# Rotary embedding on one core: x's first megabyte ahead of sin on the sync queue, and the first tile in fewer pieces

## The chip, the cores and the metric

The kernel runs on one core of a Trainium2 chip. The metric is the device time of one execution in microseconds, the median over the runs. Every time inside an execution comes from one profiled execution and is counted from the start of its span.

## The reference

`x` has the shape (8, 2048, 8, 64): batch, sequence, heads, head size, in float32. `cos` and `sin` have the shape (2048, 32). The two halves of each head are rotated by the tables of their position:

```python
x1 = x[..., : x.shape[-1] // 2]
x2 = x[..., x.shape[-1] // 2 :]
cos = cos[None, :, None, :]
sin = sin[None, :, None, :]
out1 = x1 * cos - x2 * sin
out2 = x1 * sin + x2 * cos
return np.concatenate([out1, out2], axis=-1)
```

The input and the output are 33.55 MB each, and each table is 256 KB.

## The kernel before

**Tiles.** A partition q holds the 16 positions 16q to 16q + 15, so the tables lie on the chip as 128 rows of 16 x 32 values (2 KB in each partition). One batch entry is cut into two slabs of 8 positions. A slab is 128 x 4096 float32, which is 2 MB in rows of 16 KB. There are 16 slabs: the first half of the positions for all 8 batch entries, then the second half. `HD` is 512, the values of one position; `UNIT` is 4 positions or 2048 values; `SLAB` is 4096.

**Loads.** `load(i)` issues slab i's load on the sync queue (SP). `cuts(i)` says in how many transfers: slab 0 in four (256 KB, 256 KB, 512 KB and 1 MB), all others in one. Ten slabs have a buffer (`NBUF`). In front of all of this the sync queue issues the load of `sin_sb` (L86) and the scalar queue (ACT) the load of `cos_sb` (L87). Loads 10 to 15 are issued inside the main loop, each when the buffer of the slab ten places earlier has been stored.

**Tables.** ScalarE writes `nsin`, the negative of sin (L91). VectorE (DVE) copies cos into PSUM as `cos_ps` (L92).

**Work on one piece.** `rotate(i, lo, n)` takes n values of a slab. `pieces(i)` says how slab i is cut for this: slab 0 into 512, 512, 1024 and 2048, the last slab into 2048, 1024, 512 and 512, all others into two units of 2048. For each piece

- GpSimd (POOL) writes `t2` with two multiplications on half of the values each (L107): the first halves of the heads by sin, then the second halves by nsin. A piece of 2048 is therefore 1024 elements in each of the two. There are three buffers of `t2`, in SBUF.
- DVE multiplies the piece by cos into `t1` (L112; one buffer, in PSUM), and adds `t2` to it, writing over the piece of x (L117).

When a slab is done, ACT issues its store (L127), as one transfer of 2 MB; the last slab is stored piece by piece.

**Order.** The engines run side by side, and each one works through its own instructions in a fixed order, waiting on semaphores for its inputs and free buffers. That order is set when the program is built, and can differ from the order of the calls in the source where two instructions don't depend on each other. On the DMA side, sync carries all loads but cos, and scalar carries cos and all stores.

Of the kernel before, what the change touches and what calls it, by code (L numbers as in the profile page):

```python
# [2 lines left out]

# [4 lines left out]


@with_exitstack  # L10
def kernel(
    ctx: ExitStack,
    tc: tile.TileContext,
    x: bass.AP,
    cos: bass.AP,
    sin: bass.AP,
    out: bass.AP,
):
    nc = tc.nc
    f32 = mybir.dt.float32  # L20
    PSUM = bass.MemoryType.PSUM

    B, S, H, D = x.shape
    Dh = D // 2
    P = 128
    HD = H * D
    R = S // P

    SL = 8
    n_half = R // SL  # L30
    SLAB = SL * HD
    UNIT = 4 * HD
    NBUF = 10

    xv = x.rearrange("b (q r) h d -> b q (r h d)", q=P)
    ov = out.rearrange("b (q r) h d -> b q (r h d)", q=P)
    cos_src = cos.rearrange("(q r) d -> q r d", q=P)
    sin_src = sin.rearrange("(q r) d -> q r d", q=P)

    const_pool = ctx.enter_context(tc.tile_pool(name="const", bufs=1))  # L40
    tab_pool = ctx.enter_context(tc.tile_pool(name="tab", bufs=1, space=PSUM))
    t1_pool = ctx.enter_context(tc.tile_pool(name="t1p", bufs=1, space=PSUM))
    xpool = ctx.enter_context(tc.tile_pool(name="xpool", bufs=NBUF))
    t2_pool = ctx.enter_context(tc.tile_pool(name="t2p", bufs=3))

    cos_sb = const_pool.tile([P, R, Dh], f32, tag="cb")
    sin_sb = const_pool.tile([P, R, Dh], f32, tag="sb")
    nsin = const_pool.tile([P, R, Dh], f32, tag="ns")
    cos_ps = tab_pool.tile([P, R, Dh], f32, tag="cp")

    slabs = [(b, l) for l in range(n_half) for b in range(B)]
    last = len(slabs) - 1
    xts = {}

    def cuts(i):
        if i == 0:
            return [HD, HD, 2 * HD, UNIT]
        return [SLAB]

    def pieces(i):  # L60
        if i == 0:
            return [HD, HD, 2 * HD, UNIT]
        if i == last:
            return [UNIT, 2 * HD, HD, HD]
        return [UNIT, UNIT]

    def stores(i):
        return pieces(i) if i == last else [SLAB]

    def spans(sizes):  # L70
        lo = 0
        for n in sizes:
            yield lo, n
            lo += n

    def load(i):
        b, l = slabs[i]
        xt = xpool.tile([P, SLAB], f32, tag="xt", name=f"xt{i}")
        for lo, n in spans(cuts(i)):
            nc.sync.dma_start(  # L80
                out=xt[:, lo : lo + n],
                in_=xv[b, :, l * SLAB + lo : l * SLAB + lo + n],
            )
        xts[i] = xt

    nc.sync.dma_start(out=sin_sb, in_=sin_src)  # L86
    nc.scalar.dma_start(out=cos_sb, in_=cos_src)  # L87
    for i in range(NBUF):
        load(i)

    nc.scalar.mul(nsin, sin_sb, -1.0)  # L91
    nc.vector.tensor_copy(cos_ps, cos_sb)  # L92

    def rep(a, n):
        return dataclasses.replace(a, ap=[a.ap[0][:], a.ap[1][:], [0, n], a.ap[-1][:]])

    def rotate(i, lo, n):
        b, l = slabs[i]
        xt = xts[i][:, lo : lo + n]
        r0 = l * SL + lo // HD  # L100
        nr = n // HD
        t1 = t1_pool.tile([P, n], f32, tag="t1")
        t2 = t2_pool.tile([P, n], f32, tag="t2")
        xu = xt.rearrange("p (g u d) -> p g u d", u=2, d=Dh)
        t2u = t2.rearrange("p (g u d) -> p g u d", u=2, d=Dh)
        for u, tab in ((1, sin_sb), (0, nsin)):
            nc.gpsimd.tensor_mul(  # L107
                out=t2u[:, :, u, :].rearrange("p (r h) d -> p r h d", h=H),
                in0=xu[:, :, 1 - u, :].rearrange("p (r h) d -> p r h d", h=H),
                in1=rep(tab[:, r0 : r0 + nr, :], H),  # L110
            )
        nc.vector.tensor_mul(  # L112
            out=t1.rearrange("p (r k d) -> p r k d", r=nr, d=Dh),
            in0=xt.rearrange("p (r k d) -> p r k d", r=nr, d=Dh),
            in1=rep(cos_ps[:, r0 : r0 + nr, :], 2 * H),
        )
        nc.vector.tensor_add(out=xt, in0=t1, in1=t2)  # L117

    for i, (b, l) in enumerate(slabs):
        done = 0  # L120
        st = list(spans(stores(i)))
        for lo, n in spans(pieces(i)):
            rotate(i, lo, n)
            done = lo + n
            while st and st[0][0] + st[0][1] <= done:
                slo, sn = st.pop(0)
                nc.scalar.dma_start(  # L127
                    out=ov[b, :, l * SLAB + slo : l * SLAB + slo + sn],
                    in_=xts[i][:, slo : slo + sn],
                )  # L130
        if i >= 1 and i - 1 + NBUF <= last:
            load(i - 1 + NBUF)


# [1 line left out]
_INS = ['x', 'cos', 'sin']  # L136
_OUTS = [((8, 2048, 8, 64), 'float32')]


# [23 lines left out]
```

## Time and profile before

| what | value |
|---|---|
| median of 11 runs | 164.64 us (164.48 to 165.02) |
| profiled execution | 164.66 us |
| its span | 162.9 us |
| DVE busy | 148.8 us in 73 instructions |
| POOL busy | 147.7 us in 76 instructions |
| bytes moved by DMA | 67.65 MB, 415 GB/s over the span |
| sin, issue to landing | 0.74 to 4.44 us |
| cos, issue to landing | 0.73 to 4.63 us |
| x's first 256 KB, issue to landing | 1.16 to 5.15 us |
| first POOL multiply of the main work | 5.29 us |
| last DVE add ends | 159.99 us |

The span is the part of the execution in which the profiler sees work; the rest of the device time lies around it. A share of busy time is an average over the whole span. In a list of instructions, each line gives the start, the duration, the engine, the line in the kernel, the operation, what is written from what, the shapes, and in brackets how long the engine had stood idle and for what. POOL's durations run a little into the next instruction, so the distance from one start to the next is the better measure of its pace.

### The profile page before, as it was taken

To read this page: it belongs to the slowest core of one execution; us is meant where nothing else is said; L and a number is where in the kernel's file an instruction comes from. 1 tells how busy PE (TensorE), PEld (TensorE's weight loads), DVE (VectorE), ACT (ScalarE), POOL (GpSimd) and SP (SyncE) were. 2 spreads that over 40 slices of the span, in tenths; PEclk is the share of its full clock that TensorE was granted. 3 is DMA by queue.
4 is the path that set the end of the run, shared out by engine and by line. 5 is a ranking of instruction groups with operands and counts; after the bars stand their busy time and mean duration, and the time that the engine had idled before them with its cause. 6 is when DMAs were issued, how large, how long until landed. Compare 5 with 4: busy or idle time off the path is not lost.

```text
span 162.9 us, 331 instructions
## 1 busy us (share of the span) xinstructions
DVE 148.8 (91%) x73; ACT 1.9 (1%) x2; POOL 147.7 (91%) x76
## 2 busy tenths in 40 slices
DVE  0687999999999999999999999999999999999992
ACT  3100000000000000000000000000000000000000
POOL 0799999999999999999999999999898998989820
DMA  4999999999999999999999999999999999999995
GB/s 151 418 449 422 410 378 422 431 439 427 422 447 418 426 443 439 422 431 437 426 422 447 422 422 445 431 422 435 439 426 422 447 418 431 439 435 418 439 397 198
DMA packets 5762, 67.65 MB, mean 415 GB/s; under 512 B 640, under 2 KB 640, under 8 KB 1664
## 3 DMA queue, kind: packets, MB, share of 16 engines
q1 hardware_dynamic: 2880, 33.82, 49.5%
q10 hardware_dynamic: 2880, 33.82, 48.7%
q14 instruction: 2, 0.02, 0.0%
HBM read 34.08 MB, written 33.55 MB: 415 GB/s over the span
## 4 chain that ended last, share of the span: by engine, by line
DVE 87%; POOL 6%; DMA 2%; issue 2%; DVEq 0%; SPq 0%; POOLq 0%
DVE xt L117 44%; DVE t L112 43%; POOL t L107 6%; DMA xt<-in_x_dram 2%; DVEq L117 0%; SPq L86 0%; POOLq L107 0%
## 5 line engine op out<-in xcount | busy, mean ns | idle before, releaser
L107 POOL TENSOR_TENSOR t<-xt,sin_sb 128x1024 f32<-128x1024 f32 (+2 forms) x36 | 75.3, 2091 | 7.9 <-DMA xt<-in_x_dram 7.1
L117 DVE TENSOR_TENSOR xt<-t,t 128x2048 f32<-128x2048 f32 (+2 forms) x36 | 74.0, 2055 | 5.4 <-POOL t L107 2.0
L107 POOL TENSOR_TENSOR t<-xt,nsin 128x1024 f32<-128x1024 f32 (+2 forms) x36 | 75.4, 2093 | 0.0
L112 DVE TENSOR_TENSOR t<-xt,cos_ps 128x2048 f32<-128x2048 f32 (+2 forms) x36 | 74.1, 2058 | 1.2
L92 DVE COPY cos_ps<-cos_sb 128x512 f32<-128x512 f32 x1 | 0.7, 695 | 4.6 <-DMA cos_sb<-in_cos_dram 4.6
L91 ACT ACT_TABLE_LOAD x1 | 1.3, 1283 | 1.2 <-PEq L147 1.2
L91 ACT ACTIVATE nsin<-sin_sb 128x512 f32<-128x512 f32 x1 | 0.6, 630 | 2.0 <-DMA sin_sb<-in_sin_dram 2.0
L147 POOL MEMSET const-float32-0.0<- 128x1 f32 x1 | 0.1, 98 | 0.2 <-issue 0.2
L147 POOL MEMSET const-bfloat16-1.0<- 128x1 bf16 x1 | 0.1, 101 | 0.0
L147 POOL MEMSET const-uint8-127<- 128x1 uint8 x1 | 0.1, 101 | 0.0
L147 POOL MEMSET const-float32-1.0<- 128x1 f32 x1 | 0.1, 98 | 0.0
## 6 DMA issues: line engine op xcount, KB each, us to landing
xt<-in_x_dram SPq DMA_DIRECT2D x15, 2048.0 KB, 47.6
out_dram<-xt ACTq DMA_DIRECT2D x15, 2048.0 KB, 15.7
xt<-in_x_dram SPq DMA_DIRECT2D x1, 1024.0 KB, 7.4
out_dram<-xt ACTq DMA_DIRECT2D x1, 1024.0 KB, 4.8
xt<-in_x_dram SPq DMA_DIRECT2D x2, 256.0 KB, 4.3
xt<-in_x_dram SPq DMA_DIRECT2D x1, 512.0 KB, 5.4
out_dram<-xt ACTq DMA_DIRECT2D x1, 512.0 KB, 3.5
out_dram<-xt ACTq DMA_DIRECT2D x2, 256.0 KB, 2.3
```

The source lines that it names most:

```text
L91: nc.scalar.mul(nsin, sin_sb, -1.0)
L92: nc.vector.tensor_copy(cos_ps, cos_sb)
L107: nc.gpsimd.tensor_mul(out=t2u[:, :, u, :].rearrange("p (r h) d -> p r h d", h=H), in0=xu[:, :, 1 - u, :].rearrange("p (r h) d -> p r h d" ...
L112: nc.vector.tensor_mul(out=t1.rearrange("p (r k d) -> p r k d", r=nr, d=Dh), in0=xt.rearrange("p (r k d) -> p r k d", r=nr, d=Dh), in1=rep ...
L117: nc.vector.tensor_add(out=xt, in0=t1, in1=t2)
L147: nc = _bacc.Bacc("TRN2", target_bir_lowering=False, num_devices=1)
```

## The change

Slab 0 is loaded in two transfers of 1 MB, whose rows are 8 KB. The first of them is the first transfer on the sync queue; sin follows it there, and the second 1 MB comes after sin. cos is still the first transfer on the scalar queue. The first half of slab 0 is worked in two pieces of 1024 instead of pieces of 512, 512 and 1024; its second half stays one piece of 2048. All other slabs, the stores and the buffers are as before.

```diff
     def cuts(i):
         if i == 0:
-            return [HD, HD, 2 * HD, UNIT]
+            return [UNIT, UNIT]
         return [SLAB]
 
     def pieces(i):
         if i == 0:
-            return [HD, HD, 2 * HD, UNIT]
+            return [2 * HD, 2 * HD, UNIT]
         if i == last:
             return [UNIT, 2 * HD, HD, HD]
         return [UNIT, UNIT]
...
                 in_=xv[b, :, l * SLAB + lo : l * SLAB + lo + n],
             )
+            if i == 0 and lo == 0:
+                nc.sync.dma_start(out=sin_sb, in_=sin_src)
         xts[i] = xt
 
-    nc.sync.dma_start(out=sin_sb, in_=sin_src)
     nc.scalar.dma_start(out=cos_sb, in_=cos_src)
     for i in range(NBUF):
         load(i)
```

## The prediction

> **What bounds the kernel now.** I read the page first: busy shares, then the chain that ended last.
>
> ```profile
> span 162.9 us, 331 instructions
> DVE 148.8 (91%) x73; ACT 1.9 (1%) x2; POOL 147.7 (91%) x76
> ...
> DMA  4999999999999999999999999999999999999995
> ...
> DVE 87%; POOL 6%; DMA 2%; issue 2%; DVEq 0%; SPq 0%; POOLq 0%
> ...
> xt<-in_x_dram SPq DMA_DIRECT2D x1, 512.0 KB, 5.4
> ```
>
> DVE, POOL and the DMA engines are all near full, so shares don't decide. The chain does: 87% of the span hangs on DVE. The chain in order of time shows what comes ahead of DVE:
>
> ```profile
> 1.16 3.99 DMA xt<-in_x_dram
> ...
> 5.29 4.72 POOL t L107 x6
> ...
> 10.43 4.62 POOL t L107 x2
> ...
> 15.07 2.30 DVE xt L117
> ```
>
> From 15.07 us (the add of slab 0's second half) to 159.99 us DVE has no gap over 0.1 us. Each unit of 2048 costs it 4.73 us (add to multiply 2.33, multiply to add 2.40: 17.40, 19.80, 22.12 in the timeline); POOL needs 4.57 for the same unit. So **whatever moves the add at 15.07 moves the end by as much**, unless something else becomes the bound. That add waits for POOL, which starts at 5.29, when x's first 256 KB lands (5.15).
>
> The timeline gives the pitches of the start:
>
> ```profile
> 4.45 0.63 ACT L91 ACTIVATE nsin<-sin_sb 128x512 f32<-128x512 f32 x1 [2.00 <-DMA sin_sb<-in_sin_dram]
> 4.62 0.69 DVE L92 COPY cos_ps<-cos_sb 128x512 f32<-128x512 f32 x1 [4.62 <-DMA cos_sb<-in_cos_dram]
> ...
> 9.22 1.26 POOL L107 TENSOR_TENSOR t<-xt,nsin 128x512 f32<-128x512 f32 x1
> 10.43 2.33 POOL L107 TENSOR_TENSOR t<-xt,sin_sb 128x1024 f32<-128x1024 f32 x1
> 10.51 1.22 DVE L117 TENSOR_TENSOR xt<-t,t 128x1024 f32<-128x1024 f32 x1 [0.31 <-POOL t L107]
> 11.77 2.29 DVE L112 TENSOR_TENSOR t<-xt,cos_ps 128x2048 f32<-128x2048 f32 x1
> 12.70 2.33 POOL L107 TENSOR_TENSOR t<-xt,nsin 128x1024 f32<-128x1024 f32 x1
> ...
> 15.07 2.29 DVE L117 TENSOR_TENSOR xt<-t,t 128x2048 f32<-128x2048 f32 x1 [1.01 <-POOL t L107]
> ```
>
> A POOL multiply on 512 elements comes every 1.22 us (9.22 to 10.43 is 1.21, 7.99 to 9.22 is 1.23), one on 1024 every 2.28. A DVE add on 1024 is followed after 1.26 us (10.51 to 11.77); multiply to add on 1024 takes 1.33 (154.39 to 155.72, last slab).
>
> The DMA by stretches, with columns stretch, its length, busy time of DVE, ACT and POOL, clock, DMA share and GB/s:
>
> ```profile
> 2.00:2.50 0.50, 0.00 (x0) 0.44 (x1) 0.00 (x0) 1.00 0.12 16
> 2.50:3.00 0.50, 0.00 (x0) 0.00 (x0) 0.00 (x0) 1.00 0.81 311
> 3.00:3.50 0.50, 0.00 (x0) 0.00 (x0) 0.00 (x0) 1.00 1.07 414
> 8.00:10.00 2.00, 1.86 (x3) 0.00 (x0) 2.00 (x3) 1.00 1.05 446
> ```
>
> Data begins at about 2.6 us (311 GB/s in that half microsecond is 0.39 us at 400). The tables and x's first rows, all 2 KB, run at 400 GB/s; the larger rows after them at 435 to 446.
>
> **What the Trainium skill says.** (1) "DMA: Bandwidth & Descriptors", section "Queues, rings and completion order": each engine consumes one issuer's descriptors in ring order and alternates between the rows of different issuers; an increment lands only after that engine's earlier writes. The trace agrees: between 3.0 and 3.5 us the sync and scalar queues take about equal shares, and sin and cos land together (4.44 and 4.63), ahead of x. (2) The same page, "Issuing engines are not separate DMA queues": transfers from both queues share the 16 engines, a second issuer saves only issue time. Here a SyncE issue takes 0.37 to 0.43 us. (3) "VectorE: DVE Perf Modes", the section on the TRN2 errata: a fixed cost per instruction besides the elements. Here the add on 512, 1024 and 2048 takes 692, 1224 and 2292 ns: 1068 ns for 1024 elements, so 0.16 us fixed.
>
> **The change part by part.**
> *Transfers.* POOL's first multiply needs x's first piece and sin. Before, 0.79 MB (sin, cos, 256 KB of x) are ahead of its start. After, sin stands in the sync ring behind 1.05 MB of x, and cos, on the other ring, gets its turns meanwhile: 1.57 MB. The nearest row is the 512 KB piece of before, which lands when exactly the same 1.57 MB are through: issued at 2.1, 5.4 us to landing, at 7.5. From the rates: 2.61 + 1.05/0.435 (2.41) + 0.52/0.40 (1.31) = 6.33, plus the lag from the modelled last byte to landing. That lag is 0.52 for sin (3.92 by rate, 4.44), 0.57 for the first piece of x (4.58, 5.15), 0.95 for the second (5.24, 6.2), 1.0 for the third (6.5, 7.5); the share of the engine that finishes last is in it. I take 0.85: sin lands at 7.2. POOL starts 0.14 after landing (5.15, 5.29): **T = 7.3**. Bounds: 5.7 if x alone held it (2.61 + 2.41 + 0.55 + 0.14); 7.8 with 400 GB/s throughout and a lag of 1.1.
>
> *POOL.* Four multiplies on 256 and two on 512 (5.29 to 10.43: 5.14 us) become four on 512 (4.88): 0.26 less. In the changed kernel's built order both halves' sin multiplies stand ahead of both nsin multiplies. That costs POOL nothing (three t2 buffers), but the first DVE add now waits for POOL's third instruction: T + 2.44 + 1.26 + 0.04 = T + 3.74. POOL's end of the second half: T + 4.88 + 2.28 + 2.33 = T + 9.49.
>
> *DVE.* Four instructions of 0.70 us on 512 become two of 1.23 on 1024. It is one queue in order: add a at T + 3.74; multiply b 5.00; add b 6.33; multiply of the second half 7.59; its add at 7.59 + 2.40 = **T + 9.99**. POOL is done at 9.53 by then, so DVE itself binds here, where before it stood idle for 1.01 us. With the pairs alternating as written it would be T + 9.53.
>
> *What costs nothing.* cos: at the latest with x's first piece (6.3), its copy (0.69) and the first multiply (1.33) end by 8.4, before add a at 11.0. nsin: ScalarE starts at 7.2, done 7.85, needed at T + 2.44 = 9.7; behind it on the scalar queue stands only the first store, due near 19.6. x's second 1 MB: by the row of before (10.0, the same 2.62 MB through) it is there ahead of T + 4.88 = 12.2. SyncE issues two transfers fewer. Its next wait for a free semaphore moves from slab 3's load (for sin, 4.44) to slab 4's (for cos, about 6); three slab loads of 2 MB stand in the ring by then, some 14 us of transfer at 437 GB/s, so the DMA engines don't run dry. These covers would have to fail by over 2 us.
>
> *Sum.* The add moves from 15.07 to 7.3 + 9.99 = 17.3: **2.2 us later**. Downstream nothing absorbs it: DVE has no gap to give. The later stores let loads run ahead, so the four waits of POOL of 0.55 us on loads near the end shrink; but POOL is off the path there (done 149.94, DVE's add at 152.06), so that is no gain. The profiled execution took 164.66 (span 162.9 and 1.8 around it), the median of 11 is 164.64: 166.85.
>
> **The rivals.**
> *The end is set by bytes.* For it: the DMA row reads 9 in 38 slices, and POOL waits for loads near the end. Then a late DVE start is absorbed, and 1.05 MB in 8 KB rows instead of 2 and 4 KB gains 1.05/0.40 − 1.05/0.435 = 0.2 us: 164.45, not slower. It decides only if stores are still backed up when DVE ends:
>
> ```profile
> 158.00:160.00 2.00, 1.86 (x3) 0.00 (x0) 0.00 (x0) 1.00 0.96 386
> 160.00:162.90 2.90, 0.00 (x0) 0.00 (x0) 0.00 (x0) 1.00 0.31 115
> ```
>
> After 160.0 they are mostly idle, and the last 256 KB store lands in 2.0 us, the shortest of all transfers. Against it, then. If half were absorbed, 165.75.
> *Sin is not held behind x.* If the engines mixed one ring's transfers, sin would come near 5 us, x alone would set T at 5.7, and the add comes at 15.7: 0.6 later, 165.3. The second x piece landing a microsecond after the first in before speaks against it.
> *A later landing.* One slow engine, carrying a share of both rings, could hold sin's last increment: a lag of 1.8 gives T = 8.3 and 167.85. The lags seen grow from 0.5 to 1.0 with the bytes ahead, so it isn't excluded.
>
> **How the numbers follow.** The first case 0.80 (166.85; with T from 6.6 to 7.8, 166.1 to 167.4), bytes 0.06 (a third of it a gain of over 0.2%), sin free 0.08, later landing 0.06. About 0.2% (0.33 us) is what a measurement here can tell from no change. Faster 0.02, same 0.05 (the rest of bytes, a little of sin free), slower 0.93. The range runs from 165.3 (sin free) to 167.7, and leaves out bytes and most of later landing.
>
> **What would show it.** In the changed profile: sin landing near 7.2 and ScalarE's nsin there; POOL's first multiply at 7.3; the first add on 1024 at 11.0; the add of the second half at 17.3 with almost no idle ahead of it; then DVE gapless to about 162.2 and the last store 2.3 us on. I am wrong if POOL starts before 6.5, if the add of the second half waits for POOL, or if the last DVE add is later by clearly less than the first one is.

## The result and the profile after

The changed kernel takes 166.80 us (median of 8 runs, 166.56 to 167.00) against 164.72 us (31 runs): a ratio of 1.0125, with a 95% interval of 1.0116 to 1.0134. That is 2.1 us slower, where 2.2 was forecast. The profiled execution took 166.70 us with a span of 164.9, 2.0 longer than the span of before.

The page of the changed kernel (busy time, share and instructions; then DVE and POOL in 40 slices; the chain by engine and by line):

```profile
span 164.9 us, 321 instructions
DVE 148.4 (90%) x71; ACT 1.9 (1%) x2; POOL 147.2 (89%) x74
...
DVE  0449999999999999999999999999999999999992
...
POOL 0299999999999999999999999999999999999120
...
DVE 89%; DMA 3%; POOL 2%; issue 2%; DVEq 0%; SPq 0%; POOLq 0%
DVE xt L118 45%; DVE t L113 44%; DMA sin_sb<-in_sin_dram 3%; POOL t L108 2%; DVEq L118 0%; SPq L80 0%; POOLq L108 0%
```

Both engines do 0.4 to 0.5 us less work than before, and the span is 2 us longer: the loss is idle time. It lies in the second slice of POOL and the second and third of DVE; from the fourth slice on both rows read 9 up to the tail. The transfer at the head of the chain was x; now it is sin. The chain of the changed kernel in order of time (start, length, what):

```profile
0.74 0.36 SPq L80
1.10 0.05 issue
1.15 5.74 DMA sin_sb<-in_sin_dram
...
7.03 3.69 POOL t L108 x3
...
10.74 1.24 DVE xt L118
...
12.00 1.24 DVE t L113
...
13.33 1.24 DVE xt L118
...
14.59 2.31 DVE t L113
...
16.99 2.30 DVE xt L118
```

POOL has only three instructions in it. From 10.74 on the chain is DVE alone, where in before POOL held it up to 15.07. The timeline of the same stretch shows why:

```profile
6.44 0.69 DVE L93 COPY cos_ps<-cos_sb 128x512 f32<-128x512 f32 x1 [6.44 <-DMA cos_sb<-in_cos_dram]
6.91 0.63 ACT L92 ACTIVATE nsin<-sin_sb 128x512 f32<-128x512 f32 x1 [4.46 <-DMA sin_sb<-in_sin_dram]
7.03 2.47 POOL L108 TENSOR_TENSOR t<-xt,sin_sb 128x512 f32<-128x512 f32 x2 [6.58 <-DMA sin_sb<-in_sin_dram]
...
9.46 2.47 POOL L108 TENSOR_TENSOR t<-xt,nsin 128x512 f32<-128x512 f32 x2
10.74 1.23 DVE L118 TENSOR_TENSOR xt<-t,t 128x1024 f32<-128x1024 f32 x1 [2.34 <-POOL t L108]
...
16.99 2.29 DVE L118 TENSOR_TENSOR xt<-t,t 128x2048 f32<-128x2048 f32 x1
```

Two sin multiplies run ("x2" joins two instructions in one line), then two nsin, so DVE's first add waits 2.34 us for POOL's third instruction, and DVE stays late. The add of the second half carries no wait for POOL any more (1.01 us in before). From its start, DVE ends 144.92 us later in both kernels: 15.07 to 159.99, and 16.99 to 161.91.

### The profile page after: what moved, and what is told of

Read it like the earlier page. It is cut to its first block, busy times and chain, and to the rows that moved or that the text cites. A ratio compares the mean times of both kernels' runs of the same rounds, so it can differ in the third digit from the quotient of the medians.

```text
span 164.9 us, 321 instructions
## 1 busy us (share of the span) xinstructions
DVE 148.4 (90%) x71; ACT 1.9 (1%) x2; POOL 147.2 (89%) x74
## 4 chain that ended last, share of the span: by engine, by line
DVE 89%; DMA 3%; POOL 2%; issue 2%; DVEq 0%; SPq 0%; POOLq 0%
DVE xt L118 45%; DVE t L113 44%; DMA sin_sb<-in_sin_dram 3%; POOL t L108 2%; DVEq L118 0%; SPq L80 0%; POOLq L108 0%
```

## The experiments

The question of all of them: does the end follow from **T**, POOL's first multiply, set by the bytes ahead of it, plus the fixed run of work from T to the add of the second half of slab 0, sent on whole by DVE (theory A)? The rivals are the coarser pieces (B), sin's place behind x (C), an end set by the DMA engines (D) and by POOL (E). Each trace gives three numbers: T, the distance from T to that add, and the distance from the add's start to DVE's end. "MB ahead" counts the bytes of the transfers that theory A puts ahead of T. Each ratio is to executions of the kernel before that were timed together with that kernel; their medians lie between 164.63 and 164.72.

| kernel | MB ahead | T | T to that add | add to DVE's end | median, us | ratio, 95% interval |
|---|---|---|---|---|---|---|
| before | 0.79 | 5.29 | 9.78 | 144.92 | 164.72 | |
| changed | 1.57 | 7.03 | 9.96 | 144.92 | 166.80 | 1.0116 to 1.0134 |
| loads only | 1.57 | 7.36 | 10.55 | 144.92 | 167.40 | 1.0143 to 1.0171 |
| pieces only | 1.05 | 5.84 | 9.49 | 145.32 | 165.32 | 1.0021 to 1.0044 |
| sin ahead | 1.57 | 6.94 | 9.47 | 144.92 | 166.14 | 1.0065 to 1.0093 |
| small x, then sin | 0.79 | 5.60 | 9.78 | 144.93 | 165.11 | 1.0010 to 1.0027 |
| DVE twice | 0.79 | 5.10 | 9.78 | 147.25 | 167.20 | 1.0138 to 1.0168 |
| POOL twice | 0.79 | 5.01 | 9.99 | 145.12 | 164.79 | 0.9994 to 1.0010 |
| half tables | 0.52 | 4.13 | 10.88 | 145.46 | 165.65 | 1.0043 to 1.0085 |
| half tables, cos behind x | 0.39 | 4.44 | 10.81 | 145.13 | 165.45 | 1.0027 to 1.0060 |
| changed, whole half | 1.57 | 6.99 | 9.36 | 145.33 | 166.48 | 1.0094 to 1.0124 |
| cos behind x, slab 1 halved | 0.52 | 4.73 | 10.27 | 144.92 | 164.87 | 1.0002 to 1.0020 |

### Loads only

```diff
 # from the changed kernel
 def pieces(i):
     if i == 0:
-            return [2 * HD, 2 * HD, UNIT]
+            return [HD, HD, 2 * HD, UNIT]
```

> The changed loads (1 MB of x, then sin) with the pieces of before (512, 512, 1024, 2048). Theory A (bytes ahead of POOL's first multiply, then the order of the pieces, sent on one to one by DVE): POOL starts at 7.03 as in the changed kernel. The built order puts three sin multiplies ahead of three nsin, so the first add waits until T + 3.3, DVE then works 2 x 1.52 + 2.59 us and the second half's multiply, and its add comes at T + 10.5 = 17.6: 2.5 us later than in before, 167.2 us. Rival B (the pieces of 1024 are what costs, not the loads): the time goes back to before, 164.7. Rival C (sin's place behind x costs all, pieces nothing): as the changed kernel, 166.8.

Measured: 167.40. The finer pieces don't bring the time back; with these loads they make it worse, because the build puts three sin multiplies ahead of three nsin. The distance of 10.55 is the one worked out (10.5). B falls as the main cause. T is 7.36 here and 7.03 in the changed kernel, with the same transfers in the same order.

### Pieces only

```diff
 # from the kernel before
 def cuts(i), pieces(i), slab 0:
-            return [HD, HD, 2 * HD, UNIT]
+            return [2 * HD, 2 * HD, UNIT]
```

> Sin first as in before; the first half of slab 0 loaded and worked in two pieces of 1024 (512 KB each), the second half as one. Theory A: 1.05 MB is ahead of POOL's first multiply, which the row of before's second piece puts at a landing of 6.1 to 6.2, so T = 6.3; POOL alternates sin and nsin here, so the second half's add comes at T + 9.53 = 15.8, 0.75 later than in before: 165.4. Rival B (pieces cost all): 166.8. Rival C (sin's place costs all): 164.7.

Measured: 165.32, near the 165.4 of theory A, but by other terms, so that the agreement is luck. T is 5.84, not 6.3, so the add comes only 0.26 later than in before. The other 0.4 is a stall of DVE, in the timeline of this kernel:

```profile
79.08 2.29 DVE L112 TENSOR_TENSOR t<-xt,cos_ps 128x2048 f32<-128x2048 f32 x1
...
81.88 2.29 DVE L117 TENSOR_TENSOR xt<-t,t 128x2048 f32<-128x2048 f32 x1 [0.51 <-DVE t L112]
```

From multiply to add it takes 2.80 us here, 2.40 in its other units. The chain calls 0.45 us of it "issue": nothing that the profile records was waited for. A second trace of the same kernel:

> The kernel with only the pieces changed once more. Its first trace had DVE stand still for 0.51 us at 81.4, with both inputs of the add done. If that belongs to the kernel, it is there again; if it is an accident of one execution, DVE's end comes 144.92 us after the start of the second half's add.

T was 5.89, and the stall was there again, at 81.94 and of the same length, with the end 145.33 after the add. So it belongs to the program, not to one execution. Without it this kernel would take about 164.9, an estimate from the 0.41 us.

### Sin ahead of x's megabyte

```diff
 # from the changed kernel
-            if i == 0 and lo == 0:
-                nc.sync.dma_start(out=sin_sb, in_=sin_src)
...
+    nc.sync.dma_start(out=sin_sb, in_=sin_src)
     nc.scalar.dma_start(out=cos_sb, in_=cos_src)
```

> The changed kernel with sin put back ahead of x on the sync queue; x's two transfers of 1 MB and the pieces stay. Theory A: still 1.57 MB ahead of the first multiply, only the last one to land is now x; T = 6.9 to 7.1. What changes is POOL's order, which alternates again, so the add of the second half comes at T + 9.53 = 16.5: 1.5 later than in before, 166.2, and 0.5 ahead of the changed kernel. Rival C (sin's place behind x costs all): T near 5.3, 164.7 to 165.

Measured: 166.14. The timeline of this kernel:

```profile
4.25 0.63 ACT L91 ACTIVATE nsin<-sin_sb 128x512 f32<-128x512 f32 x1 [1.80 <-DMA sin_sb<-in_sin_dram]
...
6.94 1.25 POOL L107 TENSOR_TENSOR t<-xt,sin_sb 128x512 f32<-128x512 f32 x1 [6.50 <-DMA xt<-in_x_dram]
8.15 1.25 POOL L107 TENSOR_TENSOR t<-xt,nsin 128x512 f32<-128x512 f32 x1
...
16.41 2.29 DVE L117 TENSOR_TENSOR xt<-t,t 128x2048 f32<-128x2048 f32 x1 [0.83 <-POOL t L107]
```

sin is there 2.66 us earlier (nsin at 4.25 instead of 6.91) and POOL starts at almost the same time (6.94 and 7.03): the same 1.57 MB are ahead of it, and now x is last to land. C falls as the main cause. What the place of sin does change is POOL's order, which alternates again: 9.47 instead of 9.96. That is 0.49 of the 0.66 us between the two medians.

### x's small piece, then sin

```diff
 # from the changed kernel, slab 0
 def cuts(i):
-            return [UNIT, UNIT]
+            return [HD, HD, 2 * HD, UNIT]
 def pieces(i):
-            return [2 * HD, 2 * HD, UNIT]
+            return [HD, HD, 2 * HD, UNIT]
```

> The changed order of issues (x's first piece ahead of sin) with the transfers and pieces of before (256, 256, 512 KB, 1 MB). Theory A: 0.79 MB ahead of the first multiply as in before, sin the last to land: T = 5.2 to 5.4, 164.7, no change beyond 0.2 us. Rival C (sin behind x costs, whatever the size of x's transfer): 0.5 us or more above before, 165.2 to 166.

Measured: 165.11, which is 0.2 to 0.4 us above before, so this expectation missed. T is 5.60, against 5.01 to 5.29 in the three traces with the transfers of before, and the 0.31 by which it is later than in before arrives whole at the end. With equal bytes ahead, sin second in the ring (a queue's row of waiting transfers) lands somewhat later here than x second in the ring. One trace's T could be scatter, but the median of 21 runs is later too. So a small share of C is real. Why is open: the DMA engines moved 370 GB/s between 2.5 and 5.0 us here and 385 to 392 in traces of the old order, which is worth 0.10 to 0.14 us by an estimate from these rates.

### DVE's and POOL's work doubled in one place

```diff
 # both from the kernel before; slab 8, second unit
+        for _ in range(2 if i == 8 and lo == UNIT else 1):
             nc.vector.tensor_mul(...)
 # and, in the other kernel
-        for u, tab in ((1, sin_sb), (0, nsin)):
+        for u, tab in ((1, sin_sb), (0, nsin)) + (((0, nsin),) if i == 8 and lo == UNIT else ()):
```

> The kernel before, with DVE's cos multiply of slab 8's second unit issued twice (the same t1 written twice, 2.3 us more of DVE near 86 us). Theory A (DVE sets the end, with nothing to absorb a delay): 2.3 us more, 167.0. Rival D (the end is set by the bytes that the DMA engines move, and DVE has slack against them): 164.7 to 165.5.

> The kernel before, with POOL's nsin multiply of slab 8's second unit issued twice (the same t2 written twice, 2.3 us more of POOL near 86 us). POOL leads DVE by 2.7 us there. Theory A: nothing, 164.7 to 164.9. Rival E (POOL is the bound, or DVE and POOL slow each other): 1 to 2.3 us more, 165.7 to 167.

Measured: 167.20 for DVE and 164.79 for POOL. One more multiply of DVE moves its end by 2.33 us (147.25 against 144.92), all of it; one more of POOL moves the median by nothing that can be measured. D falls for a delay of DVE, and E falls. Both traces also show how close the loads stand. With POOL's work doubled T was 5.01, and POOL then waited 0.29 us for slab 1 at 15.26; DVE waited 0.27 us behind it at 19.90, long before the added multiply near 86 us, and that makes the 145.12. With DVE's work doubled POOL waited 0.53 us for a slab at 97.67, and its result was ready only just as DVE came to the add at 102.26. For this reason the chain of that trace runs through loads for 58% of the span, though DVE lost nothing there.

### The changed kernel with its first half in one piece

```diff
 # from the changed kernel
 def pieces(i):
     if i == 0:
-            return [2 * HD, 2 * HD, UNIT]
+            return [UNIT, UNIT]
```

> The changed kernel with the first half of slab 0 worked as one piece of 2048 instead of two of 1024; loads and sin's place stay. Theory A (part of the loss is POOL's order sin, sin, nsin, nsin, which holds DVE's first add to T + 3.7 and makes DVE itself late): POOL alternates again; the first add is at T + 4.65, the second half's multiply at T + 6.98, its add at T + 9.38 instead of T + 9.96: 0.6 less than the changed kernel, 166.2. Rival F (cutting the first half lets DVE start earlier and helps, so the coarser piece costs): 166.8 or more. T itself has been 7.03 and 7.36 in two executions with these loads.

Measured: 166.48. At the start it goes as worked out: T to the add is 9.36 (9.38 expected), 0.6 less than in the changed kernel. But DVE stalls again, ahead of the add at 87.63, by 0.41 us, so that most of the 0.6 is lost again. The intervals of the two ratios overlap; it is the trace's distance, 9.36 against 9.96, that speaks against rival F: the cut into halves costs, through POOL's order.

A second trace of the changed kernel shows how far T strays with nothing changed:

> The changed kernel once more, for a second trace of the same loads. Theory A: T between 6.9 and 7.4, and whatever T is, the second half's add at T + 9.96 and DVE's end 144.92 us after that add begins.

Measured: T = 7.45, a little outside; the add at T + 9.96 = 17.41; DVE's end at 162.33, again 144.92 after the add. This execution took 167.13 us. In the four traces with these loads, T is 6.99, 7.03, 7.36 and 7.45.

### Trying for less: fewer bytes ahead of the first multiply

If bytes ahead cost time, fewer should gain. Three kernels, all from the one before, with their edits in short:

```diff
 # half tables: 8 of the 16 positions first, the rest behind slab 3
+    nc.sync.dma_start(out=sin_sb[0], in_=sin_src[:, 0:SL, :])
+    nc.scalar.dma_start(out=cos_sb[0], in_=cos_src[:, 0:SL, :])
 # half tables, cos behind x: sin's half on scalar, then on sync
+    x[first 256 KB], cos_sb[0], x[the rest]
 # cos behind x, slab 1 halved: the same order with whole tables, and
+        if i == 1:
+            return [UNIT, UNIT]
```

> The kernel before with each table cut into the 8 positions of the first eight slabs, loaded where the whole table was, and the 8 positions of the last eight slabs, loaded on the sync queue behind slab 3 and prepared on ScalarE. Theory A: 0.52 MB instead of 0.79 MB is ahead of POOL's first multiply, 0.26/0.40 = 0.65 us less: T = 4.65, 164.0. Rival C (only what stands in sin's place matters, not the bytes): T 5.1 or later, 164.5 and up. Rows of 1 KB may move slower, which would take up to 0.3 of the gain.

> As the kernel with the tables in halves, and in addition sin's half first on the scalar queue, x's first 256 KB first on the sync queue, cos's half behind it. Theory A: 0.39 MB ahead of POOL's first multiply, each transfer first on its own ring: T = 4.3, 163.7. cos lands near 4.6 and is ready for DVE's first multiply at about 5.1, ahead of the first add at T + 1.4. If cos comes over 0.5 us later than that, DVE's first add waits, but the second half's add still waits for POOL, so the end doesn't move.

> The kernel before with sin first on the scalar queue, x's first 256 KB first on the sync queue, cos behind it, and slab 1 loaded in two transfers of 1 MB. Theory A: 0.52 MB ahead of POOL's first multiply, T = 4.6 to 4.8; then x's third piece (7.5 to 7.9 in all runs so far) holds POOL, so that its second half ends near 14.7 instead of 15.05; slab 1's first half lands near 12.5 and can't hold POOL at 15.3 as in the kernels with halved tables. The second half's add comes 0.3 earlier: 164.4. If the DMA engines, 96% busy until DVE's end in before, give nothing away at the end, 164.7.

Measured: 165.65, 165.45 and 164.87. None beats before. T came down (4.13, 4.44 and 4.73, where 4.65, 4.3 and 4.6 to 4.8 were expected), but the add of the second half hardly moved (15.01, 15.25, 15.00). The waits in the timeline of the kernel with half tables:

```profile
4.13 0.72 POOL L110 TENSOR_TENSOR t<-xt,sin_sb 128x256 f32<-128x256 f32 x1 [3.69 <-DMA xt<-in_x_dram]
...
7.88 1.25 POOL L110 TENSOR_TENSOR t<-xt,sin_sb 128x512 f32<-128x512 f32 x1 [0.99 <-DMA xt<-in_x_dram]
...
15.27 2.33 POOL L110 TENSOR_TENSOR t<-xt,sin_sb 128x1024 f32<-128x1024 f32 x1 [0.29 <-DMA xt<-in_x_dram]
...
105.32 2.29 DVE L120 TENSOR_TENSOR xt<-t,t 128x2048 f32<-128x2048 f32 x1 [0.38 <-POOL t L110]
```

POOL starts 1.16 us earlier and then waits for x's third piece and for slab 1. Its multiply on the third piece starts at 7.88, 8.09 and 7.84 in the three kernels, no earlier than the 7.82 to 7.99 of the traces with the transfers of before. In the windows of the kernel with half tables (columns as in the prediction) the DMA moves less than the 385 and 418 GB/s of before in the same two windows:

```profile
2.50:5.00 2.50, 1.12 (x2) 0.42 (x1) 0.87 (x2) 1.00 0.98 318
5.00:7.50 2.50, 1.80 (x3) 0.00 (x0) 1.89 (x3) 1.00 1.00 339
```

The 1 KB rows of the halved tables are not shown to be the reason: with whole tables and cos behind x there are none, and the same windows have 343 and 363 GB/s.

The last line of the timeline above is new: near 105 us DVE itself waits for POOL, which had waited for loads. Another 0.3 to 0.4 us of both kernels with half tables lies behind DVE's end: their span ends 3.3 and 3.2 us after it, 2.9 in before. Why is open. With slab 1 halved the wait for it is gone, and the third piece still holds POOL (until 7.84). **So T sets the end only down to about the T of before**; below that the arrival of x does. That was not in theory A at first. Two of the expectations leave it out, and the third has it too small: the add 0.3 earlier, where it was 0.07. These kernels also show that bytes are not the whole of T: 0.52 MB gave 4.13 with both tables first and 4.73 with x first on its queue, and 0.39 MB with x first gave 4.44. Row sizes and queues differ there as well. With "small x, then sin" (5.60 against 5.01 to 5.29) and the changed kernel (6.99 to 7.45 in four traces, against 6.94 with sin ahead) this is the same sign four times: at equal or fewer bytes, POOL starts later where x goes first. The cause is not shown.

## Why the prediction was right, point by point

- *What bounds the kernel.* Right, and shown from both sides: 2.33 us more on DVE is 2.33 us at its end, 2.3 us more on POOL is nothing. The 144.92 us from the second half's add to DVE's end are the same to 0.01 us in before, the changed kernel (twice), loads only, sin ahead and small x, then sin.
- *Transfers.* 1.57 MB ahead of POOL's first multiply was the right quantity in the main: with sin first it starts at 6.94, with sin second at 6.99 to 7.45. The Trainium skill, in "DMA: Bandwidth & Descriptors", section "Queues, rings and completion order", has each DMA engine take the work of one ring in order and turn between the rings. The trace agrees: sin, issued at 1.15 behind 1.05 MB in its ring, landed at 6.89, after x's first piece (6.23); cos, on the other ring, by 6.44. The section also has an engine drain a whole packet of about 9 to 17 descriptors before it turns to the other ring. Here the turns look shorter, as the last section shows.
- *The size of T.* 7.3 was said and 7.03 measured in the profiled execution, 6.99 to 7.45 over four. The term that was off is the lag after the modelled last byte, taken at 0.85: 6.89 less the modelled 6.33 is 0.56, like the first transfers of before (0.52 and 0.57). In the other traces it is up to 0.98. So the lag was within what occurs, and agreement of the sum to 0.1 us is closer than a guess of this lag could promise: that much is luck.
- *POOL's order and DVE's queue.* T + 3.74 for the first add (3.71 measured) and T + 9.99 for the second half's add (9.96), with DVE the one that binds. Sin ahead, which alternates, shows 9.47 (9.53 was said), so the order costs 0.49 of the 2.1.
- *What costs nothing.* All covers held: cos at 6.44, nsin at 6.91 with its first use at 9.46, x's second megabyte landing at 9.4. POOL's waits for loads near the end are gone, and that brought nothing, as said.
- *The rivals.* The end set by bytes did not absorb the delay. Sin free of x didn't occur. Of a later landing there is only the scatter, up to T = 7.45, not the full microsecond (8.3).

The sum in the profiled executions: T + 1.74, T to the add + 0.18, together 1.92 at DVE's end. The span grew by 2.0, since 0.1 us more lies after DVE's end. The median grew by 2.1; it lies 0.1 us above the profiled execution, which a T of about 7.1 would explain, an estimate well inside the 6.99 to 7.45 of the four traces.

## What to carry to other kernels

Ahead of the first instruction of the engine that starts the chain, count first the bytes that must have passed on all queues, and only then the place of one transfer: here moving the first chunk to the front cost time, most of it because the chunk grew to four times its size. Follow the engine that sets the end to the last point where it still waits; a delay there arrives whole, and a gain there arrives only until the next arrival is late. Read the built order of instructions too, since a table that is late by one transfer turned the order of another engine around and cost 0.5 us.

## What the hardware showed that was not expected

- DVE stood still for 0.41 us once in each trace of two kernels (pieces only, twice at the same instruction, at 81.88 and 81.94; whole half at 87.63), with both inputs done. By count it is DVE's 35th instruction in both kernels. Sin ahead and the changed kernel have the same list of DVE operations as pieces only and don't show it. A fetch of instructions is an obvious suspect, and the profile has such transfers (queue 14, 8 KB). But in pieces only the one nearest to the stall runs between 85 and 86 us, after the stall, and the changed kernel has one between 86.5 and 87.5 and no stall. So no wait for such a transfer shows, and what the stall is stays open.
- The same transfers in the same order land up to 0.46 us apart from one execution to the next (sin at 6.85 to 7.31 in four traces).
- Two rings seem to share the engines by turns of one row: between 3.0 and 3.5 us the changed kernel's sync ring (8 KB rows) moved 20 packets of one row each and its scalar ring (2 KB rows) 18, and from 2.5 to 5.0 us they moved 93 and 96. So the ring with larger rows got four fifths of the bytes. The counts are of all 16 engines together; the order on one engine is not in the record. The columns are packets, MB and share of the engines' time, from 3.0 to 3.5 us:

```profile
q1 hardware_dynamic: 20, 0.16, 83.3%
q10 hardware_dynamic: 18, 0.04, 18.9%
```
